# Low halves of split weight blocks: an adding DMA in place of a subtraction

## The chip, the cores and the metric

The kernel runs on one core of one Trainium2 chip. The metric is the device time of one execution in microseconds (us). Below, PE is the matrix engine, PEld its weight loads, DVE the vector engine, ACT the scalar engine, POOL the GpSimd engine, and SP the engine whose queue issues the DMAs.

## The reference

The reference runs two layers of a transformer-like trunk over 128 context tokens and 512 latent tokens with 1024 channels. In each layer, cut to what matters here:

```
h = rmsnorm(x) * (1 + sc1) + sh1
bg, cg, xin, q, k, v, cf_u, ga, gb, gc = split(h @ w_in)          # 1024 -> 8704
y_a = (bg * dwconv3(cg * xin)) @ sc_w_out
y_b = diff_attention(q, k, v) @ attn_w_out                        # 8 heads, two softmaxes each
y_c = silu(layernorm(dwconv31(za * sigmoid(zg)))) @ cf_w_out
m = sigmoid(ga) * y_a + sigmoid(gb) * y_b + sigmoid(gc) * y_c
x = x + gt1 * rmsnorm(m @ w_o)
h = rmsnorm(x) * (1 + sc2) + sh2
x = x + gt2 * rmsnorm(square(relu(h @ w_ff1)) @ w_ff2)            # 1024 -> 4096 -> 1024
```

All of it is float32. The six modulation vectors (sc, sh, gt) of each layer are products of two conditioning rows with a 1024 x 6144 matrix.

## The kernel before

Channels lie on the partitions and the 640 tokens in the free dimension. The operands of the large products are of type float32r, and every such product is made of three: a number is split into a high half (its rounding to float32r) and a low half (what the rounding left), and high by high, high by low and low by high are summed in PSUM.

The weights come in blocks of 128 partitions by 1024 float32 (512 KB). `wblock` (line 590) makes a block ready: SP loads it into a tile `raw`, ACT rounds it into `wh`, and DVE or POOL subtracts `wh` from `raw` into `wl`. There are three buffers of `raw`, shared with the weights of the modulation vectors, and five each of `wh` and `wl`:

```
NW = 5
NRAW = 3
```

`gemm` (line 597) then issues for each of eight slices of 128 channels the three products over the tokens, two halves of 320 tokens for a whole projection, so that a block feeds 48 matrix products. `first` issues four blocks side by side, slice by slice, for one part of the tokens: this happens where a sub-layer's end and the next one's start overlap, and at the kernel's start. `v_pair` takes the weights as the moving operand.

The order of the instructions is made by a list scheduler when the kernel is built (`Recorder`): the operations are traced, given costs (`cost`), priorities (`rank`) and starts (`schedule`), and each engine then issues its own in the order of those starts. Tiles are taken from their pools in that order. Operations called on `nc.either` go to DVE or to POOL, whichever the scheduler expects to end first. On POOL there are also the powers that make `rsqrt` of the token statistics (`stat` and `subln`). At run time each engine goes through its list in order, and waits where an operand isn't there.

Of the kernel before, what the change touches and what calls it, by code (L numbers as in the profile page):

```python
# [51 lines left out]
# a conv tile's width: context and latent tokens with zeros between them  # L52
UW = T + PAD
# tiles: working ones, split weight blocks, weight blocks as loaded
# [3 lines left out]
# order of the instructions: how far ahead it looks, and the slack given to what may wait  # L58
# [5 lines left out]
# conv taps to a head  # L64
NTAP = 6
# parts of the tokens: columns of the first, and of the first at the very end
TP = 2 * P
TPL = 3 * P
# tiles whose squares are summed ahead of the matrix product, by part
NRES = (5, 4)  # L70
# last blocks of a second part that have a PSUM tile of their own
TAILS = 2
# tiles of the first layer's shift and scale that TensorE makes
# [7 lines left out]
# ---- order of the instructions  # L81
# The kernel is traced into a list of operations. A list scheduler, with the engines' rates, puts every engine's
# operations into the order in which they are then issued; tiles are taken from their pools in that order.
# [14 lines left out]
class View:  # L98
    """A view of a tile: what is done to its access pattern, and the elements that it covers."""
# [25 lines left out]
    def rows(self, r0, r1):  # L125
        """rows of a matrix in DRAM, strung together, on every partition."""
        n = (r1 - r0) * self.el.shape[1]
        return View(self.buf, np.broadcast_to(self.el[r0:r1].reshape(1, n), (P, n)),
                    self.steps + (lambda x: x[r0:r1, :].rearrange("a b -> (a b)")[None, :].to_broadcast([P, n]),))
# [40 lines left out]
# microseconds from an operation's end to the start of one that waits for it, by the two engines  # L170
# [15 lines left out]
class Recorder:  # L186
    def __init__(self, nc):
        self.nc = nc
        self.ops = []
        self.group = None  # L190
        self.late = 0
        for e in ("tensor", "vector", "scalar", "gpsimd", "sync"):
            setattr(self, e, Engine(self, e))
        # operations for either of two engines
        self.either = Engine(self, "vector", "gpsimd")

    def cost(self, eng, method, outs, ins, kw, args):
        """microseconds that an engine is held."""
        def n(v):
            return int(np.prod(v.shape[1:]))  # L200

        psum = any(v.buf.psum for v in outs + ins)
        m = max(n(v) for v in outs[:1] + ins)
        if eng == "tensor":
            c = n(outs[0]) + 6
            if method == "transpose":
                c = 260
            elif ins[0].buf.dt == F32:
                m4 = 4 * outs[0].shape[0]
                c = max(4 * c - 12, m4 if self.group is not None and self.group.calls else m4 / 2)  # L210
            elif c < 230:
                c = 230
            self.last = c, min(c, 4 * n(outs[0])) * ins[0].shape[0] / P
            return c / 2400
        if eng == "vector":
            if method == "reciprocal":
                return 0.065 + m / 120
            if not psum and method in ("tensor_copy", "tensor_scalar"):
                return 0.065 + m / 1920
            return 0.067 + m / 960 + (0.062 if method == "scalar_tensor_tensor" else 0)  # L220
        if eng == "scalar":
            c = (0.053 if psum else 0.095) + m / 1200
            if "accum_out" not in kw and any(isinstance(kw.get(x), View) for x in ("bias", "scale")):
                c += 0.092
            return c + 0.19 if "accum_out" in kw else c
        if eng == "gpsimd":
            if ALU.pow in (kw.get("op"), kw.get("op1")):
                return 0.1 + m * 0.2
            if method == "memset":
                return 0.1 + m / 900  # L230
            return 0.155 + m * 2.1e-3
        return 0.06

    def add(self, eng, method, args, kw, other=None):
# [9 lines left out]
        if eng == "sync":  # L244
            sz = (outs + ins)[0].shape
            nbytes = 4 * int(np.prod(sz))
# [11 lines left out]
        if nbytes:  # L258
            op.acts = ("dma", nbytes)
        if eng == "scalar":  # L260
            fn = [a.name for a in rest if isinstance(a, AF)]
            op.acts = SETS.get(fn[0]) if fn else None
# [49 lines left out]
    def rank(self):  # L312
        """priorities: the latest start that lets TensorE go on without a pause, in its order of the program."""
# [17 lines left out]
        for op in reversed(self.ops):  # L331
            d = op.dur
            if op.eng == "sync":
                d = 1.3 + op.acts[1] / 360e3
            for u in op.users:
                op.prio = min(op.prio, u.prio - d - lat(op.eng, u.eng))
# [3 lines left out]
    def schedule(self):  # L340
        """the operations in the order of their starts."""
# [17 lines left out]
        # operations that use each tile, to know when it is free  # L359
# [25 lines left out]
        def soon(e, op, start):  # L385
            """whether a late operation should let one go first that is about to be ready."""
# [31 lines left out]
        def pe_time(op, t):  # L418
            """duration on TensorE, whose clock doubles after a tick of enough work."""
# [12 lines left out]
        while len(seq) < n:  # L432
# [48 lines left out]
            if e == "sync":  # L481
                gen[0] = max(start, gen[0]) + 0.65
                dma[0] = max(gen[0] + 0.65, dma[0]) + op.acts[1] / 360e3
                op.end = dma[0]
            else:
# [35 lines left out]
def trunk_kernel(ctx: ExitStack, tc: tile.TileContext, xT, crow, ccol, wmod, wmod0, win, wv, wa, wc, wattn, wo, wff1, wff2,  # L521
# [34 lines left out]
    def f(ap):  # L556
        return ap.bitcast(F32)
# [5 lines left out]
    # token ranges of a half by group (0: context, 1: latent)  # L563
    SEG = [[(0, TC, 0), (TC, TH, 1)], [(TH, T, 1)]]
    # the parts in which one sub-layer's end and the next one's start overlap
# [5 lines left out]
    # ---- constants  # L571
# [12 lines left out]
    # ---- weights  # L584
# [5 lines left out]
    def wblock(src, eng=None):  # L590
# [4 lines left out]
        (eng or nc.either).tensor_sub(wl, r, f(wh))  # L595
        return wh, wl

    def gemm(outs, wb, rhs, ks, koff=0):
        """outs: [(psum ap, c0, c1)]; rhs[k] = (hi, lo)."""
# [31 lines left out]
    def first(wbs, rhs, hf):  # L631
        """products of four blocks with one part of the tokens, in step with the tiles of rhs."""
# [21 lines left out]
    def sums(ss, c0, c1, w, pos=None):  # L654
        """sums over channels, tokens on partitions; w: the column of 1/n for the mean."""
# [16 lines left out]
    # ---- per-token statistics: means over channels, or rsqrt of them and eps, to a broadcast  # L672
# [22 lines left out]
    def sq_acc(acc, src, a, b, first):  # L695
        """acc[:, a:b] (+)= src^2"""
# [7 lines left out]
    def modulate(x, sq, G, B, h, hf):  # L704
        """h[k] = hi, lo of x*rstd*G + B on a part of the tokens."""
# [11 lines left out]
    def squares(src, a, b, ss, k, n, eng=nc.either):  # L717
        """squares, the first n tiles' summed."""
# [7 lines left out]
    def residual(xs, m, sq, hf, need, part):  # L726
        """m = xs + m * rstd; returns the squares of the new m."""
# [17 lines left out]
    # ---- modulation  # L745
# [12 lines left out]
    def cond():  # L758
        """silu of the two conditioning rows, on every partition, in halves."""
# [7 lines left out]
    def modvec(l, st, j, cb):  # L767
        """chunk j of the modulation vectors, a tile at a time."""
# [27 lines left out]
    # ---- start: the first layer's scale and shift a tile at a time, each followed by its products  # L796
# [64 lines left out]
    for l in range(DEPTH):  # L861
# [6 lines left out]
        # ---- Conformer conv branch: gated input, first two channel tiles half by half  # L868
# [5 lines left out]
        def pos(t):  # L874
            """column of a token: context and latent are parted by zeros."""
            return t if t < TC else t + PAD

        def conv(g, j):
            """depthwise products, a tap at a time."""
# [44 lines left out]
        # ---- lambda  # L924
# [12 lines left out]
        # ---- attention  # L937
# [38 lines left out]
        def rope(pt, out, scale):  # L976
            """rotary embedding of the latent part of a projection into out; returns the projection."""
# [17 lines left out]
        def k_head(hd):  # L995
            """keys: (high parts twice over the partitions for each map, low parts), and the context's as they are."""
# [12 lines left out]
        def q_head(hd):  # L1009
            """queries, scaled: for each map its high part on its own partitions and the low part on the others."""  # L1010
# [7 lines left out]
        def softmax(S, n, view, s0):  # L1018
            """S: two psum views [q, n keys]; returns s0 * (p0 - lam p1) as a tile, s0 the sum under p0."""
# [17 lines left out]
        def three(out, A, B, start, stop):  # L1037
            """out (+)= A.T @ B from (hi, lo) pairs."""
# [30 lines left out]
        def values(aa, ac, v, vc):  # L1069
            """weights @ v of the latent and the context queries, channels on partitions; s0 times the output."""  # L1070
# [24 lines left out]
        def subln(o, s0, hd):  # L1095
            """the output, and what its queries are to be scaled by: rsqrt of the mean square and eps, times s0."""
# [20 lines left out]
        # ---- short gated conv branch  # L1117
# [69 lines left out]
        # ---- modulation vectors that are needed later  # L1187
# [8 lines left out]
        # ---- merge of the branches  # L1196
        def gated(gate, n):
            """sigmoids of the gates, n channel tiles ahead."""
# [10 lines left out]
        def pair(wsrc):  # L1209
            """a block holds the products of two channel tiles."""  # L1210
# [19 lines left out]
        # ---- layer norm and silu of the conv branch  # L1230
# [22 lines left out]
        # ---- attention output  # L1253
# [38 lines left out]
        # ---- output projection, residual, second norm  # L1292
        def tail(blk, rhs, ks, base, xsrc, E, need, mid=None, PART=PART, PSEG=PSEG):
            """last products of a sub-layer, first part of the tokens ahead of the second, and the residual."""
# [73 lines left out]
        # ---- MLP in chunks of hidden channels  # L1368
# [73 lines left out]
# ---- host layout  # L1442
def _blocks(w):
    """[K, M] -> [M/128, 128, K]: block m holds [p, k, c] = w[k*128+p, m*128+c]."""
# [4 lines left out]
def _pairs(w):  # L1449
    """blocks of half the depth, two to a tile."""  # L1450
# [107 lines left out]
```

## Time and profile before

| | |
|---|---|
| median of 2 runs | 2607.17 us (2605.89 to 2608.45) |
| span of the profiled execution | 2606.3 us |
| PE busy | 2527.0 us, 97% |
| PEld busy | 2459.4 us, 94% |
| DVE busy | 1663.9 us, 64% |
| ACT busy | 991.9 us, 38% |
| POOL busy | 329.0 us, 13% |
| DMA, share of 16 engines | 30.8%, 271.14 MB on the queue that SP feeds |

The span runs from the first to the last instruction of one execution. A share is an average over stages that have different limits; where the engines wait is read from the views by stage.

### The profile page before, as it was taken

Reading aid. Unit: us, or ns where it says so; the run is one execution under the profiler, and the core shown is the slowest. Engines: PE = TensorE matmul, PEld = TensorE weight load, DVE = VectorE, ACT = ScalarE, POOL = GpSimd, SP = SyncE. Lnnn points to the kernel's source line nnn. Section 1 sums busy time; section 2 is a strip of 40 time slices with the busy share of each in tenths; the row PEclk is TensorE's granted clock in tenths of the full one; section 3 lists DMA queues with packets and bytes.
Section 4 is the critical chain, followed back from the end, with each engine's and each line's share of the span. In section 5 each row is a group of like instructions: output and inputs, shape, how many; then the busy total and the mean of one; then the engine's idle time right before and its main releaser. Section 6 shows DMA issues by size and latency. Waiting matters only on the chain. (4 is left out here: it accounts for less than half of the span.)

```text
span 2606.3 us, 41673 instructions
## 1 busy us (share of the span) xinstructions
PE 2527.0 (97%) x17092; PEld 2459.4 (94%) x17092; DVE 1663.9 (64%) x2807; ACT 991.9 (38%) x1714; POOL 329.0 (13%) x218
## 2 busy tenths in 40 slices
PE   7999999999999999999989999999999999999998
PEld 7988899999999999999989888999999989999998
DVE  7699787954675886775468988787243363333325
ACT  4666553223334432222446566433232343222213
POOL 2122220001201010110012222101010020000001
PEclk9999999999999899999989999999999989999999
DMA  7322222341453554444323212123221322222231
GB/s 268 94 79 67 77 73 79 132 168 66 138 182 110 172 172 146 154 151 134 116 74 92 69 62 81 65 105 120 78 73 66 112 91 81 74 73 77 78 110 46
DMA packets 103779, 273.80 MB, mean 105 GB/s; under 512 B 13012, under 2 KB 35876, under 8 KB 103588
## 3 DMA queue, kind: packets, MB, share of 16 engines
q1 hardware_dynamic: 103588, 271.14, 30.8%
q8 instruction: 134, 2.20, 0.3%
q14 instruction: 57, 0.47, 0.1%
HBM read 244.83 MB, written 17.87 MB: 101 GB/s over the span
## 5 line engine op out<-in xcount | busy, mean ns | idle before, releaser
L517 PE MATMUL pp<-u,wh 128*128 128x320 f32 (+2 forms) x6560 | 1245.7, 310 | 13.9 <-DVE u L517 11.4
L517 PEld LDWEIGHTS pp<-u,wh 128*128 128x128 f32 x6560 | 1034.3, 189 | 17.9 <-DVE u L517 13.9
L517 PE MATMUL pp<-u,wl 128*128 128x320 f32 (+2 forms) x3280 | 764.6, 309 | 0.0
L517 PE MATMUL ps<-u,wh 128*128 128x320 f32 (+2 forms) x2912 | 664.6, 317 | 6.0 <-ACT u L517 5.3
L517 DVE TENSOR_TENSOR wl<-raw,wh 128x1024 fp32r<-128x1024 f32 x265 | 332.7, 1256 | 373.8 <-ACT wh L517 373.4
L517 PEld LDWEIGHTS pp<-u,wl 128*128 128x128 f32 x3280 | 555.6, 189 | 0.0
L517 ACT CAST wh<-raw 128x1024 fp32r<-128x1024 f32 x312 | 326.8, 1049 | 590.2 <-PE pp L517 366.9
L517 PEld LDWEIGHTS ps<-u,wh 128*128 128x128 f32 x2912 | 493.3, 191 | 16.8 <-issue 6.7
L517 PE MATMUL ps<-u,wl 128*128 128x320 f32 (+2 forms) x1456 | 456.7, 314 | 0.0
L517 DVE TENSOR_TENSOR u<-u,u 128x640 fp32r<-128x640 f32 (+8 forms) x356 | 279.4, 794 | 65.7 <-ACT u L517 52.1
L517 PEld LDWEIGHTS ps<-u,wl 128*128 128x128 f32 x1456 | 276.9, 190 | 0.0
L517 ACT ACTIVATE u<-pp 128x640 f32<-128x640 f32 (+3 forms) x124 | 79.8, 649 | 439.1 <-PE pp L517 427.7
L517 DVE CUSTOM_DVE_ANT_0 u<-raw,u 128x512 f32<-128x512 f32 x320 | 227.4, 758 | 27.6 <-DMA raw<-in_wmod_dram 25.8
L517 DVE SCALAR_TENSOR_TENSOR u<-u,par,u 128x640 f32<-128x640 f32 (+16 forms) x272 | 240.2, 891 | 3.8
L517 POOL TENSOR_TENSOR wl<-raw,wh 128x1024 fp32r<-128x1024 f32 x47 | 121.7, 2590 | 494.2 <-ACT wh L517 285.6
L517 DVE TENSOR_TENSOR u<-u,pp 128x640 f32<-128x640 f32 (+2 forms) x60 | 45.2, 754 | 182.3 <-PE pp L517 182.1
L517 ACT CAST u<-u 64x640 fp32r<-64x640 f32 (+1 forms) x152 | 110.4, 727 | 121.3 <-DVE u L517 107.1
L517 ACT ACTIVATE u<-u 128x640 fp32r<-128x640 f32 (+5 forms) x200 | 117.5, 600 | 83.6 <-DVE u L517 67.6
L517 POOL TENSOR_TENSOR u<-u,u 128x384 f32<-128x384 f32 (+4 forms) x59 | 88.7, 1514 | 431.8 <-ACT u L517 227.2
L517 ACT ACTIVATE u<-pp,mx 128x640 f32<-128x640 f32 x128 | 100.9, 793 | 72.4 <-DVE mx L517 72.1
L517 PE MATMUL ps<-wh,u 128*128 128x256 f32 x640 | 122.3, 286 | 1.8 <-ACT vo L517 1.8
L517 DVE TENSOR_TENSOR u<-ps,u 128x512 fp32r<-128x512 f32 (+4 forms) x192 | 92.1, 507 | 45.2 <-PE ps L517 23.1
(91 smaller groups left out, 1839.9 us busy)
## 6 DMA issues: line engine op xcount, KB each, us to landing
raw<-in_wff_dram SPq DMA_DIRECT2D x128, 512.0 KB, 3.3
raw<-in_win_dram SPq DMA_DIRECT2D x120, 512.0 KB, 3.3
raw<-in_wmod_dram SPq DMA_DIRECT2D x80, 512.0 KB, 3.3
u<-in_wmod_dram SPq DMA_DIRECT2D x32, 256.0 KB, 6.0
raw<-in_wv_dram SPq DMA_DIRECT2D x16, 512.0 KB, 3.2
u<-u SPq DMA_DIRECT2D x128, 64.0 KB, 2.0
raw<-in_wattn_dram SPq DMA_DIRECT2D x16, 512.0 KB, 3.2
raw<-in_wo_dram SPq DMA_DIRECT2D x16, 512.0 KB, 3.3
```

The lines of the kernel that those rows point to most:

```text
L517: getattr(eng, m)(*[r(v) for v in a], **{x: r(v) for x, v in k.items()})
```

## The change

The subtraction goes. ACT writes, beside `wh`, the negated block, rounded in the same way, into `wl`; a DMA that POOL issues then reads the block from DRAM a second time and adds it onto `wl` in SBUF. The scheduler is told what such a DMA costs (1 us of POOL, and 3 us and 150 GB/s until its data are there), and that it reads its destination. The rest of the diff takes comments away, which is left out here.

```
@@ def cost
         if eng == "gpsimd":
+            if method == "dma_start":
+                return 1.0
             if ALU.pow in (kw.get("op"), kw.get("op1")):
...
@@ def add
-        if eng == "sync":
+        if method == "dma_start":
             sz = (outs + ins)[0].shape
             nbytes = 4 * int(np.prod(sz))
...
         if nbytes:
             op.acts = ("dma", nbytes)
+            if kw.get("accum_op") is not None:
+                for v in outs:
+                    self.access(op, v, False)
...
@@ def rank
             if op.eng == "sync":
                 d = 1.3 + op.acts[1] / 360e3
+            elif op.eng == "gpsimd" and op.acts is not None:
+                d = 3.0 + op.acts[1] / 150e3
...
@@ def schedule
+            elif e == "gpsimd" and op.acts is not None:
+                op.end = start + 3.0 + op.acts[1] / 150e3
             else:
                 op.end = start + dur
...
@@ def wblock
         nc.scalar.copy(wh, r)
-        (eng or nc.either).tensor_sub(wl, r, f(wh))
+        nc.scalar.mul(wl, r, -1.0)
+        nc.gpsimd.dma_start(wl, src, accum_op=ALU.add)
         return wh, wl
```

## Rows read from the trace of the kernel before

**Rows 1.** The page, its span and busy times by engine
```profile
span 2606.3 us, 41673 instructions
...
PE 2527.0 (97%) x17092; PEld 2459.4 (94%) x17092; DVE 1663.9 (64%) x2807; ACT 991.9 (38%) x1714; POOL 329.0 (13%) x218
```

**Rows 2.** Waits of PE: line, releaser, us in total, times, longest
```profile
PE ps L517 <- DVE u L517: 32.6, 30, 10.4
PE pp L517 <- DVE u L517: 13.9, 14, 4.3
PE ps L517 <- ACT u L517: 7.3, 7, 1.4
```

**Rows 3.** Groups by shape: count, busy us, mean ns, idle us before and releaser
```profile
L517 DVE TENSOR_TENSOR wl<-raw,wh 128x1024 fp32r<-128x1024 f32 x265 | 332.7, 1256 | 373.8 <-ACT wh L517 373.4
L517 ACT CAST wh<-raw 128x1024 fp32r<-128x1024 f32 x312 | 326.8, 1049 | 590.2 <-PE pp L517 366.9 <-PE ps L517 134.0 <-issue 43.6
L517 POOL TENSOR_TENSOR wl<-raw,wh 128x1024 fp32r<-128x1024 f32 x47 | 121.7, 2590 | 494.2 <-ACT wh L517 285.6 <-DVE u L517 169.6 <-PE ps L517 27.3
...
L517 POOL TENSOR_TENSOR st<-st,mhalf 128x2 f32<-128x2 f32 x8 | 7.7, 967 | 197.0 <-DVE st L517 197.0
```

**Rows 4.** ACT in order of time, steady second layer: start us, us, what
```profile
2182.27 1.05 ACT L517 CAST wh<-raw 128x1024 fp32r<-128x1024 f32 x1
...
2189.30 1.05 ACT L517 CAST wh<-raw 128x1024 fp32r<-128x1024 f32 x1
```

**Rows 5.** DMA: the queue, then issues with count, KB, us to landing
```profile
q1 hardware_dynamic: 103588, 271.14, 30.8%
...
raw<-in_wmod_dram SPq DMA_DIRECT2D x80, 512.0 KB, 3.3
...
on<-u SPq DMA_DIRECT2D x16, 320.0 KB, 2.2
```

**Rows 6.** Stretches of 50 us: busy us by engine, granted clock, DMA share, GB/s
```profile
150.00:200.00 50.00, 46.04 (x323) 40.92 (x322) 48.91 (x77) 27.41 (x62) 15.14 (x10) 1.00 0.20 64
...
900.00:950.00 50.00, 50.00 (x343) 50.00 (x342) 43.94 (x96) 18.46 (x23) 8.87 (x5) 1.00 0.60 197
...
1100.00:1150.00 50.00, 50.00 (x343) 50.00 (x342) 33.27 (x70) 9.84 (x11) 3.33 (x2) 1.00 0.45 151
...
2300.00:2350.00 50.00, 50.00 (x343) 50.00 (x342) 17.98 (x19) 13.50 (x17) 0.00 (x0) 1.00 0.22 74
```

**Rows 7.** ACT in order of time, just before the first layer's MLP
```profile
827.86 1.04 ACT L517 CAST wh<-raw 128x1024 fp32r<-128x1024 f32 x1
```

**Rows 8.** PE in order of time, start of the first layer's MLP
```profile
831.86 0.40 PE L517 MATMUL pp<-u,wh 128*128 128x256 f32 x2
...
833.16 0.28 PE L517 MATMUL pp<-u,wl 128*128 128x256 f32 x1
...
834.55 0.72 PE L517 MATMUL ps<-inv,u 128*128 128x1 f32 x6
...
846.90 5.12 PE L517 MATMUL ps<-inv,u 128*128 128x1 f32 x30 [1.07 <-DVE u L517]
```

**Rows 9.** In order of time, ACT and then PE, first head of the second layer
```profile
1356.60 1.05 ACT L517 CAST wh<-raw 128x1024 fp32r<-128x1024 f32 x1 [13.61 <-PE ps L517]
...
1362.54 0.31 PE L517 MATMUL ps<-u,wl 128*128 128x320 f32 x1
```

**Rows 10.** All engines in order of time, the kernel's start
```profile
28.00 2.55 DVE L517 TENSOR_TENSOR wl<-raw,wh 128x1024 fp32r<-128x1024 f32 x1
...
32.67 0.58 PE L517 MATMUL pp<-u,wh 128*128 128x256 f32 x1 [4.31 <-DVE u L517]
...
38.59 1.04 ACT L517 CAST wh<-raw 128x1024 fp32r<-128x1024 f32 x1
...
44.29 0.29 PE L517 MATMUL pp<-u,wl 128*128 128x256 f32 x1
```

**Rows 11.** Waits of PE from 100 to 400 us, then from 1400 to 1650
```profile
PE ps L517 <- DVE u L517: 6.4, 8, 2.0
...
PE ps L517 <- DVE u L517: 6.7, 7, 2.0
```

More of the change, by code (lines that the diff above doesn't have):

```diff
@@ L226, in cost @@
         if eng == "gpsimd":
+            if method == "dma_start":
+                return 1.0
             if ALU.pow in (kw.get("op"), kw.get("op1")):
@@ L243, in add @@
         nbytes = 0
-        if eng == "sync":
+        if method == "dma_start":
             sz = (outs + ins)[0].shape
@@ L259, in add @@
             op.acts = ("dma", nbytes)
+            if kw.get("accum_op") is not None:
+                for v in outs:
+                    self.access(op, v, False)
         if eng == "scalar":
@@ L334, in rank @@
                 d = 1.3 + op.acts[1] / 360e3
+            elif op.eng == "gpsimd" and op.acts is not None:
+                d = 3.0 + op.acts[1] / 150e3
             for u in op.users:
@@ L484, in schedule @@
                 op.end = dma[0]
+            elif e == "gpsimd" and op.acts is not None:
+                op.end = start + 3.0 + op.acts[1] / 150e3
             else:
@@ L594, in wblock @@
         nc.scalar.copy(wh, r)
-        (eng or nc.either).tensor_sub(wl, r, f(wh))
+        nc.scalar.mul(wl, r, -1.0)
+        nc.gpsimd.dma_start(wl, src, accum_op=ALU.add)
         return wh, wl
```

## The prediction

> **What bounds the kernel now.** I read the page first: PE is busy for 2527.0 of 2606.3 us [rows 1], so 79.3 us is all that better feeding can give back, 3% of the span. Then PE's own waits: those above 7 us are for tiles `u` that DVE or ACT make from activations [rows 2], 53.8 us together, and no row of that view names `wh` or `wl`. The reader is to see that today the weights are never what PE waits for. Then the groups by shape: the subtractions take 332.7 us of DVE and 121.7 us of POOL [rows 3], but by the stretches of 50 us they lie beside a PE that is busy for all 50 in three of the four rows shown [rows 6]; only in attention, the row from 150 us, is DVE itself near full, 48.91 of 50, and PE below it, 46.04. So the change takes work off an engine that is not the bound, and lengthens the way of each weight block. The question is whether that longer way stays hidden.
>
> **How far ahead a block is made.** In the steady stages ACT rounds a block every 7.03 us (2189.30 - 2182.27 [rows 4]). That is the time PE needs for one block: a buffer comes free and the next block is cast into it. With five buffers a new block has four ahead of it, 28.1 us from the start of its cast to its first use, 27.1 us from its end. Today 1.26 us of that are used by the subtraction. Wherever this pattern holds, a low half may come some 25 us later at no cost.
>
> **The new way, step by step.** From the end of the cast: (1) the negation on ACT, the cast's shape and engine, 1.05 us [rows 3]; 312 of them add 328 us to ACT's 991.9, which makes 1320 or 51%, and hide beside PE. (2) POOL's issue of the DMA. No row shows one; the ends are nothing and the shortest arithmetic on POOL, 0.97 us [rows 3]. I take 1.0, since it is POOL's own work. (3) The transfer. No row shows an adding one. A plain load of the same 512 KB lands in 3.3 us, and a read-out of 320 KB of SBUF in 2.2 us [rows 5], which is an estimated 3.5 us for 512 KB. An adding DMA reads the block and its destination and writes one; so the ends are 3.3 (a plain load) and 6.8 us (the read-out and the load one after the other). I take 6.8, as it has both to do. Sum: 1.05 + 1.0 + 6.8 = 8.9 us, with ends 4.4 and 8.9; call it 9. It fits into 27.1 three times.
>
> **What the DMA engines can carry.** Steady stage: a share of 0.22 of 50 us [rows 6] is 11.0 us, and 50 / 7.03 = 7.1 blocks, so a plain load holds all 16 engines for 1.55 us. While modulation weights are loaded too, 0.45 of 50 us gives 3.17 us for each block. Room per block: 7.03 - 1.55 = 5.48 us in the first case, 3.86 in the second. An adding DMA that costs the engines twice a plain load, 3.1 us, fits into both; 2.5 times is the limit of the second, 3.5 times that of the first. I take twice, again because two reads stand against one. The Trainium skill, Collectives: The Full Stack, Part 3 (the bandwidth ceiling), says the same in its own case: a reducing transfer there is half as fast as a copying one because each chunk needs two source reads on one ring, not because the adding costs anything. By that rule the transfers would fit and the sum below stand; no row here shows an adding transfer yet.
>
> **Where the long way shows.** Four kinds of place have less than 9 us.
> - The starts of a sub-layer, where four blocks are used side by side. The fourth block of the first MLP is cast by 828.90 [rows 7] and its low half is first used at 833.16 [rows 8]: 4.3 us. At 9 it comes 4.7 late. PE goes in order, so the sums behind it (834.55) slide too, and the residual with them; but PE waits for DVE at 846.90 anyway [rows 8], and the scheduler knows of a long transfer and can round that block sooner. Between nothing and 4.7, I take 2. There are three such starts (two MLPs, one second layer): +6.
> - The first head of the second layer: cast done at 1357.65, first use at 1362.54 [rows 9], 4.9 us, so 4.1 late. PE has no other work there: +4.
> - The kernel's start: the fourth block is cast by 39.63 and used at 44.29 [rows 10], 4.7 us, so 4.3 late. Against it, DVE spends 2.55 us on a subtraction at 28.00 just before the tile that PE awaits for 4.31 us at 32.67 [rows 10]; that goes. Net between -2.5 and +4.3: I take +1.
> - The catching up after the first MLP's start: from 900 to 950 the DMA share is 0.60 [rows 6], which leaves 20 us of 50, and 7.1 blocks at 3.1 us want 22; blocks are made up there too. Between nothing and 8, I take +4.
>
> **What comes back.** In attention PE waits 6.4 us for DVE in the first layer and 6.7 in the second [rows 11]. The subtractions there are mostly POOL's, and ACT, which makes the softmax's exponentials, gets 1.05 us more for each block. Of the 13.1 us I take a third: -4, with ends 0 and -13. At the three sub-layer starts a subtraction of 1.26 us leaves DVE's chain: between 0 and -1.26 each, I take -1 each: -3. POOL's powers, on which the statistics hang, now stand in one list with the adding DMAs, each of which waits for ACT's negation; behind such a wait stand also whatever additions POOL shares with DVE, and for them ACT and PE wait. In place of 47 subtractions of 2.59 us POOL gets 312 issues of about 1 us, in sum 329 - 122 + 312 = 519 us of 2606, and I cost the queueing at nothing, between -2 and +4. The loads on SP's queue go no later: a `raw` buffer came free after the subtraction (1.26 us after the cast) and now comes free after the negation (1.05 us). The adding DMA reads DRAM itself and holds no `raw`.
>
> **Sum.** 6 + 4 + 1 + 4 - 4 - 3 = +8 us on the span of 2606.3; the median of the runs lies 0.9 us above that span, so 2607.2 + 8 = **2615 us**. With all costs at their upper ends and no gain: 14.1 + 4.1 + 4.3 + 8 + 4 = +34. With all gains and no cost: 13.1 + 3.8 + 2.5 + 2 = -21. The forecast's own range is 2586 to 2641, and all of it lies within 2%, 2555 to 2659, about what a measurement of this kernel can tell from no change.
>
> **The rivals.**
> - *The adding DMA is rate-bound: slower.* If it holds the engines for more than 2.5 plain loads (3.86 us a block), it paces PE while modulation weights are loaded, over 80 blocks' time (80 such loads [rows 5]); the 25 us of cover then run out, since they don't come back. At 3 times, 4.65 us: 80 x (4.65 + 3.17 - 7.03) = +63, 2678 us with the terms above. At 4 times, 6.2 us: 80 x 2.34 = +187, and now the other dense stages as well, 312 - 80 - some 56 blocks of attention = 176 x (1.55 + 6.2 - 7.03) = +127, about 2929 us in all. For it: no row prices an adding transfer, and it also writes float32r from float32. Against it: two reads are two, and the queue stands at 30.8% over the span [rows 5].
> - *The way is longer than the cover in more places: little slower.* If the transfer lands at 14 us and not at 9 from the cast's end, while the rate suffices, each tight place costs 5 more and none of it is absorbed: three starts at 9.7, the head 9.1, the start of the kernel 9.3, and 4 to 8 at 900 to 950: about +50, 2657 us. For it: queues share the engines with loads; against it: the steady leads of 27 us.
> - *DVE was the real limit of the gaps: faster.* If the subtractions stood behind most of PE's waits for DVE, 32.6 + 13.9 us [rows 2], the time falls by up to 46 to 2561. Against it: in the steady stages DVE has half of its time free and PE doesn't wait at all; the waits are in chains whose other steps stay.
> - *The change doesn't do what it says:* the subtractions must vanish from DVE and POOL, since `wblock` alone makes `wl`; I give this no chance of its own.
>
> **How the numbers follow.** The forecast gets 0.63, the rate-bound DMA 0.25, the longer way 0.08, the gain 0.04. Slower by over 2% is the rate-bound case and half of the longer way, 0.29; faster by over 2% hardly any part of the last, 0.02; the rest, 0.69, is within 2%. The range goes from 2588 (some 0.05 lies below) up to 2720, which takes in a rate-bound DMA up to some 3.2 times a plain load and leaves half of that case, 0.13, above.
>
> **What would show each step.** Right: 312 casts and as many negations of about 1.05 us on ACT; no `wl` on DVE, whose busy time falls by some 330 us; a new queue with 163 MB; a share of the DMA engines in the steady stage near 0.44; landings of the adding DMA below 10 us; PE waiting for the DMA of `wl` for 5 to 20 us in all, at the starts named. Wrong: PE waiting for that DMA stage after stage, 7.03 us a block growing to 8 or more, a DMA share near 1; or PE's waits for DVE halved; or POOL busy with issues for far more than 1 us each, which would put the powers of the statistics behind them.

## The result, and the profile after

The changed kernel takes 2679.48 us, the median of 2 runs (2675.11 to 2683.84), against 2607.17 before: 1.0279 of the time, with a 95% interval of [1.0237, 1.0321], so 72 us slower. That is inside the range on record, 2588 to 2720 us, but outside the likeliest case, 2615 us and no measurable change. The range reaches so far up only because it makes room for a rival, the rate-bound DMA.

The page of the kernel after, its span, busy times and queues, to be held against [rows 1, 5]:

```profile
span 2682.1 us, 42202 instructions
...
PE 2549.4 (95%) x17092; PEld 2478.4 (92%) x17092; DVE 1300.7 (48%) x2566; ACT 1278.7 (48%) x2026; POOL 424.8 (16%) x459
...
q0 software_dynamic: 44928, 163.60, 36.0%
q1 hardware_dynamic: 103588, 271.14, 28.3%
```

DVE is rid of 363 us, ACT has the negations, and a new queue carries 163.60 MB. PE issues the same 17092 products. Its idle time grows from 79.3 to 132.7 us (span less busy), its busy time by 22.4 us at a mean granted clock of 0.976 instead of 0.985. These two are the 75.8 us by which the spans differ.

The new steps, from the groups by shape (mean ns after the comma) and the DMA issues (us to landing last), to be held against [rows 3, 5]:

```profile
L526 ACT ACTIVATE wl<-raw 128x1024 fp32r<-128x1024 f32 x312 | 331.1, 1061 | 865.5 <-PE pp L526 648.2
...
L526 POOL DMA_DIRECT2D wl<-in_wff_dram x128 | 112.2, 877 | 792.9 <-ACT wl L526 768.0
...
raw<-in_wff_dram SPq DMA_DIRECT2D x128, 512.0 KB, 6.2
wl<-in_wff_dram POOLq DMA_DIRECT2D x128, 512.0 KB, 6.7
...
raw<-in_wmod_dram SPq DMA_DIRECT2D x80, 512.0 KB, 5.1
```

The low half's own way has the size that was forecast. What has changed is the *other* transfer: a plain load landed in 3.3 us before [rows 5] and now needs 5.1 to 6.2.

Who waits, all engines (us in total, times, longest):

```profile
DVE u L526 <- DMA raw<-in_wmod_dram: 181.1, 61, 6.6
...
ACT wl L526 <- DMA raw<-in_wff_dram: 38.6, 10, 8.4
...
ACT wl L526 <- DMA raw<-in_win_dram: 28.7, 4, 9.7
PE ps L526 <- DVE u L526: 26.7, 27, 12.1
PE pp L526 <- DVE u L526: 24.9, 18, 4.0
PE pp L526 <- ACT u L526: 21.3, 12, 7.6
```

The same view of the kernel before, of all engines and then of PE:

```profile
DVE u L517 <- DMA raw<-in_wmod_dram: 25.8, 26, 3.1
...
PE pp L517 <- ACT u L517: 3.8, 9, 0.7
```

DVE's wait on modulation weights grows from 25.8 to 181.1 us. PE's own wait for a low half is 4.3 us in all (2.4 for blocks of the MLP, 1.9 for blocks of the first projection). What PE waits longer for is `u`, tiles of activations: in its products into `pp`, 21.3 us for those from ACT (3.8 before) and 24.9 for those from DVE (13.9 before [rows 2]). So the path runs from a late load through an engine that works in order to something else that this engine should have made. Here it is in the trace of the kernel after, all engines in order of time (start, duration, what, idle before and its releaser):

```profile
750.70 0.33 SPq L526 DMA_DIRECT2D raw<-in_win_dram  x1
...
760.35 1.06 ACT L526 ACTIVATE wl<-raw 128x1024 fp32r<-128x1024 f32 x1 [9.06 <-DMA raw<-in_win_dram]
761.31 0.69 ACT L526 ACTIVATE u<-pp 128x640 f32<-128x640 f32 x1
...
762.05 1.43 PE L526 MATMUL pp<-u,wh 128*128 128x320 f32 x4 [7.59 <-ACT u L526]
```

The load is issued at 750.70 and its data are there only at 760.35. ACT stands 9.06 us before the negation of that block. Behind the negation in ACT's list stands the reading out of a PSUM tile, and PE waits 7.59 us for that. It is not the block that PE waits for. The stretches around it show the DMA engines and the clock (columns as in [rows 6]):

```profile
755.00:760.00 5.00, 0.00 (x0) 0.00 (x0) 3.22 (x9) 0.00 (x0) 0.00 (x0) 0.65 1.03 301
760.00:765.00 5.00, 2.95 (x11) 2.95 (x12) 3.06 (x8) 3.21 (x4) 0.86 (x1) 0.50 0.67 189
...
1100.00:1150.00 50.00, 50.00 (x342) 50.00 (x341) 30.05 (x76) 22.66 (x28) 6.12 (x7) 1.00 0.84 221
...
2400.00:2450.00 50.00, 50.00 (x343) 50.00 (x342) 12.24 (x15) 21.55 (x26) 6.13 (x7) 1.00 0.65 149
```

While PE stands, the DMA share is 1.03; when PE starts again, its granted clock is 0.50, the lower level of 1.2 GHz, so such a pause is paid for a second time. In steady stages of both kinds (with modulation weights, 1100 to 1150; without, 2400 to 2450) PE is still busy for all 50 us.

To see where the 72 us arise I number PE's products in order, the same 17092 in every kernel (some change places, none across a limit below), and take how much later than before a stretch of them ends, less what it began with (us, one profiled execution each). The stretches are: the kernel's start (to product 600, 111.6 us in the kernel before); the first attention and its surroundings (to 4200, 649.8 us); the stretch in which 72 of the 80 blocks of modulation weights are loaded, with the first MLP (to 8400, 1274.4 us); and the second layer. The experiments below are in the same table. An entry of a few us may be chance, since 25 executions of the kernel before lie between 2602.93 and 2620.19 us.

| kernel | start | first attention | modulation weights | second layer | sum |
|---|---|---|---|---|---|
| after | +14.3 | +12.2 | +59.9 | -13.4 | +73.1 |
| e1_act_only | +1.5 | +5.0 | +3.4 | -4.1 | +5.8 |
| e2_plain_dma | +5.3 | -2.9 | +14.0 | -24.7 | -8.2 |
| e3_traffic | +5.3 | +19.4 | +21.3 | +13.6 | +59.5 |
| e4_second_layer | -1.9 | +4.3 | -0.1 | -4.0 | -1.7 |
| e5_first_layer | +10.0 | +11.6 | +61.1 | -10.2 | +72.5 |
| e6_shared_model | +16.3 | +0.5 | +39.2 | -19.0 | +37.0 |
| e7_four_raw | +15.6 | +15.9 | +23.1 | -17.2 | +37.3 |
| e8_one_mod_load | +13.1 | +6.2 | +2.7 | -12.4 | +9.7 |
| e9_order_and_raw | +20.4 | +4.3 | 0.0 | -13.9 | +10.8 |
| e10_before_four_raw | +6.0 | +2.7 | +6.5 | -0.6 | +14.5 |
| e11_second_four_raw | +7.0 | -0.3 | +6.5 | -9.7 | +3.6 |
| e12_start_subtracts | +1.4 | +0.2 | -1.4 | -17.2 | -16.9 |

The changed kernel loses most where the modulation weights stream, some at the start and in the first attention, and gains in the second layer. The rows by stretch of the lossy part, first before and then after:

```profile
649.00:1275.00 626.00, 619.82 (x4213) 617.30 (x4212) 430.98 (x883) 191.32 (x279) 76.02 (x45) 0.99 0.44 149
```

```profile
676.00:1361.00 685.00, 642.72 (x4207) 635.70 (x4206) 324.39 (x825) 270.59 (x366) 92.78 (x102) 0.95 0.76 201
```

The share rises from 0.44 to 0.76 only; PE's idle time from 6.2 to 42.3 us and its busy time by 22.9, at a clock of 0.95.

### The profile page after: what moved, and what is told of

Same layout as the page of the kernel before. It is cut to its first block, busy times and chain, and to the rows that moved or that the text cites. A ratio compares the mean times of both kernels' runs of the same rounds, so it can differ in the third digit from the quotient of the medians.

```text
span 2682.1 us, 42202 instructions
## 1 busy us (share of the span) xinstructions
PE 2549.4 (95%) x17092; PEld 2478.4 (92%) x17092; DVE 1300.7 (48%) x2566; ACT 1278.7 (48%) x2026; POOL 424.8 (16%) x459
## 3 DMA queue, kind: packets, MB, share of 16 engines
q0 software_dynamic: 44928, 163.60, 36.0%
## 5 line engine op out<-in xcount | busy, mean ns | idle before, releaser
L526 PE MATMUL pp<-u,wh 128*128 128x320 f32 (+2 forms) x6560 | 1256.5, 312 | 43.4 <-DVE u L526 22.9
L526 ACT ACTIVATE wl<-raw 128x1024 fp32r<-128x1024 f32 x312 | 331.1, 1061 | 865.5 <-PE pp L526 648.2
L526 ACT CAST wh<-raw 128x1024 fp32r<-128x1024 f32 x312 | 324.4, 1040 | 9.6 <-issue 4.8
L526 DVE TENSOR_TENSOR u<-u,u 128x640 fp32r<-128x640 f32 (+8 forms) x360 | 267.3, 750 | 120.9 <-ACT u L526 112.7
L526 DVE CUSTOM_DVE_ANT_0 u<-raw,u 128x512 f32<-128x512 f32 x320 | 204.3, 692 | 186.6 <-DMA raw<-in_wmod_dram 181.1
L526 DVE SCALAR_TENSOR_TENSOR u<-u,par,u 128x640 f32<-128x640 f32 (+16 forms) x272 | 234.6, 872 | 11.8 <-ACT u L526 6.8
L526 POOL DMA_DIRECT2D wl<-in_wff_dram x128 | 112.2, 877 | 792.9 <-ACT wl L526 768.0
L526 POOL DMA_DIRECT2D wl<-in_win_dram x120 | 105.3, 877 | 691.3 <-ACT wl L526 602.8
L526 DVE TENSOR_TENSOR u<-u 128x640 f32<-128x640 f32 (+2 forms) x68 | 51.8, 764 | 227.9 <-ACT u L526 227.7
L526 DVE TENSOR_TENSOR u<-pp,u 128x640 f32<-128x640 f32 (+1 forms) x40 | 28.5, 716 | 212.0 <-PE pp L526 197.7
```

The lines of the kernel that those rows point to most:

```text
L526: getattr(eng, m)(*[r(v) for v in a], **{x: r(v) for x, v in k.items()})
```

## The experiments

Theory A: loads land late beside the adding DMAs, and ACT and DVE, which work in order, stand on them. Rivals: B, the negation holds up ACT; C, the low half itself comes late. Within A two versions had to be told apart: that the DMA engines are simply full, or that they could carry it all and only the loads come later than the order of the instructions and three buffers allow. That the new transfers slow the instructions of the engines themselves can be ruled out by the groups by shape: DVE's reduction of modulation weights takes 692 ns after and 758 before, ACT's cast 1040 and 1049. Ratios are to the kernel before, with 95% intervals; its medians in the three groups of runs were 2609.87 (e1 to e4), 2609.67 (e5 to e8) and 2609.2 us (e9 to e12).

**e1_act_only: ACT's part alone.** ACT writes the negated block, and DVE or POOL add the weights less that; no adding DMA.

```
-        nc.gpsimd.dma_start(wl, src, accum_op=ALU.add)
+        nc.either.tensor_add(wl, r, f(wl))
```

> ACT negates each block as in the changed kernel, and DVE or POOL adds the block onto it in SBUF; there is no second read of the block and no DMA from POOL. Theory A (the DMA engines are near full while modulation weights are loaded, loads land late, and ACT and DVE stand in order on them): the traffic is that of before, so 2600 to 2620 us, DMA share near 0.22 in the steady stage. Theory B (the negation on ACT holds up ACT's other work): most of the +72 us stays, 2650 to 2690 us. Theory C (the low half's own late landing): as A, within 10 us of 2607.

Measured: 2614.37 us, 1.0017 [1.0005, 1.003]. B is worth some 4 us, not 72.

**e2_plain_dma: the same queue and waits, a plain copy.**

```
-        nc.gpsimd.dma_start(wl, src, accum_op=ALU.add)
+        nc.gpsimd.dma_start(wl, src)
```

> POOL's DMA only copies the block over the negated tile, so the low halves hold whole weights and the products are not the reference's; waits, issues and bytes read from DRAM are those of the changed kernel, only the reading of the destination is gone. Theory A: the engines are held for some 1.6 us a block in place of 3.1, the share in the stage of modulation loads falls from about 0.8 to 0.65, and most of the loss goes: 2610 to 2640 us. Theory B: no change, 2665 to 2695. Theory C: the landing shortens from 6.7 to some 4 us; of 4.3 us of waits named for it at most those go, 2670 to 2680.

Measured: 2605.98 us, 0.9981 [0.9967, 0.9995], below what theory A expected. Each engine has its instructions in the same order here as in the kernel after, so the two differ in the transfers alone. By the table that difference is worth 81 us (+73.1 against -8.2). The same bytes, over POOL's queue and with the same chain of waits, cost nothing in sum if they take the DMA engines for less time; in the stretch of the modulation weights 14.0 us stay. POOL's issue is also shorter, 0.54 us against 0.88, which this run doesn't separate; PE's waits for POOL's statistics are 5.3 us after and 5.5 before. The queue's share in this run, against 36.0% after:

```profile
q0 software_dynamic: 44928, 163.60, 21.2%
```

**e3_traffic: the kernel before, and the traffic beside it.** The subtraction stays; adding DMAs onto a scratch tile that nobody reads follow each cast.

```
         (eng or nc.either).tensor_sub(wl, r, f(wh))
+        t_ = nc.gpsimd.tensor_sub(tiny, r[:, 0:1], f(wh)[:, 0:1])
+        nc.gpsimd.dma_start(scr, src, accum_op=ALU.add).deps.add(t_)
```

> The kernel before, with its subtraction, and beside each block one adding DMA of the same 512 KB onto a scratch tile that nobody reads, issued by POOL once the block's high half is there. ACT has no negation and nobody waits for the DMA. Theory A: the loss appears although nothing waits for the adding DMA: 2640 to 2690 us, DMA share about 0.67 in the steady stage, and loads land in about 6 us. Theories B and C: 2605 to 2620 us.

Measured: 2672.21 us, 1.0232 [1.0208, 1.0256]. This speaks for A as a whole, less well than the total suggests: the table shows only 21.3 us in the stretch of the modulation weights. POOL, busy for 814.0 us here, also waits for earlier scratch transfers with the subtractions behind that wait, and 50 loads wait for the small subtraction on POOL that only this run has (120.8 us on SP's queue). I can't divide the remaining 38 us.

**e4_second_layer and e5_first_layer: one layer each.** The adding DMA where the condition holds, the subtraction elsewhere (`at[0]` is the layer whose loop runs; the second layer's first four blocks are made before it is set to 1, so they go with e5).

```
+        if at[0] == 1:      # e5: == 0
             nc.scalar.mul(wl, r, -1.0)
             nc.gpsimd.dma_start(wl, src, accum_op=ALU.add)
+        else:
+            (eng or nc.either).tensor_sub(wl, r, f(wh))
```

> The adding DMA only for the blocks made in the second layer's loop, where no modulation weights are loaded; the subtraction in the first layer and for the second layer's first four blocks. By the products' starts the changed kernel is 86 us late at the end of the first layer and 73 at the end. Theory A: no loss, and the second layer's gain of some 5 to 13 us stays: 2594 to 2605 us. Theories B and C: the second layer has 140 or so of the 312 blocks, so about half of the loss, 2635 to 2645 us.

> The other half of the run before it: the adding DMA only for blocks made up to the end of the first layer's loop, the subtraction after. Theory A: all of the loss is here, and a little more than in the changed kernel, since the second layer's gain is missing: 2680 to 2695 us. A loss that goes by the number of blocks: 2640 to 2650 us.

Measured: 2604.92 us, 0.9979 [0.9969, 0.999], for the second layer alone; 2682.79, 1.0273 [1.0248, 1.0299], for the first. All of the loss is the first layer's, and most of it (+61.1) lies where the modulation weights are loaded.

**e6_shared_model: another order.** The kernel after, but the scheduler is told that loads and adding DMAs share the engines and what an adding one costs. Nearly the same instructions (three go from DVE to POOL) in another order.

```
-                dma[0] = max(gen[0] + 0.65, dma[0]) + op.acts[1] / 360e3
+                dma[0] = max(gen[0] + 0.65, dma[0]) + op.acts[1] / 330e3
...
-                op.end = start + 3.0 + op.acts[1] / 150e3
+                dma[0] = max(start + 1.5, dma[0]) + op.acts[1] / 165e3
+                op.end = dma[0] + 1.5
```

> The changed kernel, with a scheduler that is told that the adding DMA and the loads share the engines: the adding DMA takes its bytes at 165 GB/s on the same clock as the loads, the loads go at 330 GB/s. Only the order of instructions changes. If the loss is one of order (reductions and negations put into the lists too early for loads that land late), 20 us or more come back: 2620 to 2660 us. If the engines' time is what lacks (theory A in its strict form), 2665 to 2690 us.

**e7_four_raw: a fourth buffer for loads** (`NRAW = 4`).

> The changed kernel with four buffers for loaded blocks in place of three, so that loads start earlier. If late loads come from too few of them in flight, the loss shrinks by 20 us or more: 2640 to 2660 us. If the engines are full there (theory A strict), little: 2665 to 2685 us.

Measured: e6 2642.79 us, 1.0115 [1.0086, 1.0144]; e7 2648.44, 1.0147 [1.012, 1.0173]. Either one recovers about half, with every byte still moved. So the engines are not simply full; that version of A falls.

**e8_one_mod_load: no stream of modulation weights.**

```
-            r = raw_load(wmod[l, j * KD + m])
+            r = one[0]          # one block, loaded once
```

> The changed kernel with the modulation weights' stream left out: one 512 KB block of them is loaded once and all 80 reductions read it (the modulation vectors are then wrong); reductions, adding DMAs and negations stay. Theory A: where the stream was, the share falls from about 0.8 to 0.67 and the loss there, about 60 of the 72 us, goes; start and first attention keep theirs: 2610 to 2630 us. Theories without the DMA engines' load: no change, 2665 to 2690 us.

Measured: 2625.73 us, 1.006 [1.0042, 1.0078]. The loss in that stretch goes (+2.7), with the adding DMAs all there. The start's +13.1 stays: it has another cause. This run also leaves the `raw` buffers to the weight blocks alone; that the time on the DMA engines matters with stream and buffers as they are is shown by e2.

**e9_order_and_raw: e6 and e7 together.**

> The change with both cures: the scheduler told what a load and an adding DMA cost the shared engines (that alone gave 2642.79), and a fourth buffer of raw (that alone gave 2648.44). If both cure the same thing, loads that land late, the first to act leaves the second little: 2635 to 2645. If they cure different delays, their gains of some 37 and 31 us add up in part: 2612 to 2630. If the DMA engines were simply full, neither could have gained and this would not either.

Measured: 2613.84 us, 1.0019 [1.0003, 1.0034]. The cures add up, and the stretch of the modulation weights now takes what it took before (0.0).

**e10_before_four_raw and e11_second_four_raw: what the buffer is worth without late loads.** The kernel before, and e4, with `NRAW = 4`.

> Control: the kernel before with a fourth buffer of raw. If late loads are a trouble that the adding DMAs brought, it gains the kernel before nothing: 2602 to 2612. If three buffers were too few all along, it gains 15 us or more here as well, and the fourth buffer's gain on the change says nothing of the adding DMAs.

> Adding DMAs in the second layer alone, where no modulation weights are loaded (that gave 2604.92), with a fourth buffer of raw. Late loads are not the limit there, so by the theory of late loads the buffer adds nothing: 2598 to 2608. If the buffer also helps where the engines are half free, 2590 or less.

Measured: e10 2620.29 us, 1.0035 [1.0022, 1.0048]; e11 2617.64, 1.0028 [1.0014, 1.0042], each above its expected bounds. A fourth buffer alone costs 11 us (13 in e11 against e4), by the table at the kernel's start (+6.0 in e10) and in the stretch with the first MLP (+6.5); what in the other order does it stays open. So the buffer's gain in e7 and e9 is a cure of the adding DMA's side effect, not a gain that was there for the taking. For the scheduler's new prices there is no such control: the kernel before, with loads at 330 GB/s, was not run.

**e12_start_subtracts: e9, and the first four blocks keep the subtraction** (`at[0]` starts at -1).

```
+        if at[0] >= 0:
             nc.scalar.mul(wl, r, -1.0)
             nc.gpsimd.dma_start(wl, src, accum_op=ALU.add)
+        else:
+            (eng or nc.either).tensor_sub(wl, r, f(wh))
```

> The same as the change with both cures, but the first layer's four first blocks, at the kernel's start, keep the subtraction. The change lost 10.6 us up to PE's product 300 there. If that loss is the longer way of the first low halves, it goes: some 10 us below the kernel with both cures. If it is the loads that land late there as well, little changes: within 4 us.

Measured: 2592.72 us, 0.9929 [0.99, 0.9957], 21 us below e9 and the fastest of all. The start's loss falls from 20.4 to 1.4 (e9's profiled execution was its slowest, 2621.71 us). What it was can in part be read from the kernel's start: first DMA issues from 0 to 60 us before, then after.

```profile
u<-in_crow_dram SPq DMA_DIRECT2D x4, 256.0 KB, 6.5
...
cc<-in_ccol_dram SPq DMA_DIRECT2D x1, 8.0 KB, 5.1
```

```profile
wl<-in_win_dram POOLq DMA_DIRECT2D x5, 512.0 KB, 9.0
u<-in_crow_dram SPq DMA_DIRECT2D x4, 256.0 KB, 14.2
...
cc<-in_ccol_dram SPq DMA_DIRECT2D x1, 8.0 KB, 13.0
```

The DMA share from 20 to 40 us is 1.05 both before and after: full already. Of the five adding DMAs three come in among the conditioning rows (`crow`, `ccol`), whose loads go out from 9.75 us on and take 8 us longer to land: POOL issues them at 10.50, 14.07 and 15.95 us. ACT and PE in the kernel after, in order of time:

```profile
27.06 0.21 ACT L526 ACTIVATE cc<-cc 128x16 f32<-128x16 f32 x1 [0.71 <-DMA cc<-in_ccol_dram]
...
27.33 3.58 PE L526 MATMUL ps<-cc,u 128*128 128x2 f32 x16 [6.38 <-ACT cc L526]
```

Before, that step on ACT came at 17.06. In e12 one adding DMA is left in those 60 us, at 45.27, and `crow` lands in 7.0. But the order of the loads differs too: ahead of `crow` go three blocks of weights after the change, four in e9, one in the kernel before and none in e12. In e2, whose order is that of the kernel after, `crow` lands in 10.0 and the start loses 5.3 us. So some 9 of the 14.3 us go with the longer hold of the adding DMAs, and the rest, with e9's further 6, is not divided. The low halves themselves cost PE 1.9 us of the start after the change: I had named the wrong transfer, and the expected 10 us came from the kernel after, where e9 loses more.

Last, e12 where the modulation weights stream, its waits for loads, and their landings over the run:

```profile
1050.00:1100.00 50.00, 50.00 (x343) 50.00 (x342) 28.99 (x79) 21.22 (x24) 6.92 (x8) 1.00 0.97 266
```

```profile
ACT wl L527 <- DMA raw<-in_wff_dram: 69.3, 14, 8.3
...
DVE u L527 <- DMA raw<-in_wmod_dram: 35.2, 17, 5.0
```

```profile
raw<-in_wff_dram SPq DMA_DIRECT2D x128, 512.0 KB, 6.2
...
raw<-in_wmod_dram SPq DMA_DIRECT2D x80, 512.0 KB, 6.6
```

At a share of 0.97, higher than the 0.92 that is the most in any 50 us of that stretch after the change, PE is busy for all 50 us. The loads land no sooner than after the change (6.2 us for the MLP's blocks in both, 6.6 instead of 5.1 for modulation weights), and ACT even waits longer for the MLP's blocks, 69.3 us instead of 38.6. What is gone is most of DVE's wait, 35.2 us instead of 181.1, and the loss of PE. So neither nearly full DMA engines nor late landings are a loss by themselves here; they are one where, as at 750 us after the change, work that PE soon needs stands in order behind the wait.

## Why the prediction was right or wrong

- **What bounds the kernel, and the lead of 27 us: right.** PE's wait for low halves is 4.3 us in 2682.
- **The new way, step by step: right.** Negation 1.06 us (taken 1.05), issue 0.88 (1.0), landing 6.7 (6.8). The last is right as a number only: it is a median beside other transfers, 5.5 in the steady stage from 2400 to 2450 us. No run shows an adding DMA alone, so the read-out and the load one after the other, from which I had 6.8, are not shown.
- **An adding DMA costs the engines twice a plain load: right.** 36.0% of 2682.1 us over 312 blocks is 3.09 us, against 1.55. The Trainium skill, Collectives: The Full Stack, Part 3 (the bandwidth ceiling), halves a reducing transfer's rate for its two source reads; this trace agrees on the factor, 3.09 / 1.55 = 2.0; that the second read is the reason no run here shows. The share of 0.44 that I named for the steady stage was a slip: by the same terms it is 0.22 + 7.1 x 3.1 / 50 = 0.66, and it measured 0.65.
- **"Fits into both", and "the loads on SP's queue go no later": here it failed.** As a rate the first holds (e12, 0.97). As a cost it does not. I priced when a load may go and not when it lands: I took room in the mean for no delay, and looked for delay at the low half, which has 27 us of lead. The delay came to the plain loads beside it, 3.3 to 5.1 and 6.2 us, on which DVE and ACT stand in order with little lead, and they hold back PSUM and activations. The price was +59.9 us in one stretch, where I had costed the catching up at +4. e2 (the same order, a shorter hold of the engines: +14.0), e8 (no such stream: +2.7) and e9 (another order and one more buffer: 0.0) show both ends of that chain.
- **The kernel's start, +1 (-2.5 to +4.3): the second miss, +14.3.** Again I weighed only the fourth low half's lead. The DMA engines there were full before the change (1.05), and no row of mine looked at that.
- **Sub-layer starts +6, first head of the second layer +4: wrong sign in the second layer.** From products 8400 to 9000, the second layer's start with its first head, the kernel after is 9.8 us quicker than before: PE is idle for 3.9 us (97.00 less 93.09) instead of 8.8 (108.00 less 99.25), and runs at a clock of 0.91 instead of 0.87. The stretch before, then after:

```profile
1274.00:1382.00 108.00, 99.25 (x607) 96.10 (x606) 67.28 (x145) 54.89 (x115) 16.66 (x16) 0.87 0.25 81
```

```profile
1361.00:1458.00 97.00, 93.09 (x598) 90.79 (x597) 52.37 (x134) 62.13 (x123) 21.64 (x25) 0.91 0.56 142
```

Subtractions gone from DVE's chain are worth more there than the longer way costs: from 8400 to 9000 e1, which adds in their place, gains 0.1 us, e2 10.0, and e4 and e5, which each drop a part of them, 3.7 and 5.6. The second MLP's start gains 3.4 (products 13800 to 14400), but e1 gains 3.9 there, so that this is the subtractions' is not shown. The first MLP's start lies in the stretch that loses and can't be read apart.
- **Attention -4: not seen.** The first attention's stretch is +12.2 after, -2.9 in e2 and +0.2 in e12, so it goes with a shorter hold of the DMA engines as well as with the cures; which wait carries it was not read apart.
- **The rivals.** The rate-bound DMA was nearest in size: its +63 at 3 times a plain load is close to +59.9, but by accident. Its condition, more than 2.5 times, was not met, and PE was not paced by the rate, since e12 carries the same transfers but for four blocks without loss. That the range held the measured time is therefore luck. The longer way is refuted by the 4.3 us. The gain from DVE is real, some 10 us at the second layer's start; how much of the second layer's 13 to 25 us (after, e12, e2) is due to it beyond that is not shown, since e5, which subtracts there from the fifth block on, gains 10.2, and e4, which does the opposite, 4.0.

With its two faults cured (e12) the kernel is 16 us faster than before, 2592.72 against 2609.2 us; how much of that the new order of the instructions would give without adding DMAs is not known. e9, which keeps the fault at the start, lands on 2614, beside the 2615 forecast, by a sum whose terms are others.

Open: why loads land so late at a mean share of 0.76 (whether behind single adding transfers or in short full stretches was not tried), and the fourth buffer's own cost.

## What to carry to other kernels

A DMA that is hidden itself may still cost time: ask what else is on those engines, how much later *that* lands, and who stands on it in order with what queued behind. Room in the mean is not room; check the leads of the loads that share the engines, and the stretches where the share is already near 1, the kernel's start above all. When a new transfer is added, tell the scheduler its price and move the loads ahead before judging the transfer.

## What the runs showed of the hardware

- A plain DMA from POOL's queue that writes float32r from float32 held the engines for 1.77 us a block (21.2% of 2602.9 us over 312), against 1.55 for a plain load and 3.09 for the adding one; its landing was 3.8 us against 6.7.
- The plain loads of the MLP's blocks landed later at a higher DMA share, though not by the share alone (medians of stretches of 50 us): 3.2 us at 0.22 (before, from 2300), 4.3 at 0.45 (before, from 1100), 5.5 at 0.65 (after, from 2400), 6.5 at 0.71 (e8, from 1100), 5.7 at 0.84 (after, from 1100) and 7.0 at 0.97 (e12, from 1050). PE was busy for all 50 us in each of them.
